# Gated attention in an encoder kernel: the gate weights in a tile of their own, loaded early, and the log decays written ahead of the copies of k

## The chip, the cores and the metric

One core of a Trainium2 chip runs the whole program in one launch. The metric is the device time of one execution in microseconds (us), the median of several runs. TensorE is written PE below, VectorE DVE, ScalarE ACT, GpSimd POOL and SyncE SP. SP issues nearly all transfers, from one queue, in the order in which they stand in it.

## The reference

The reference is a two-layer encoder on 512 tokens of width 1024. Layer 0 has two mixers side by side: a bidirectional diagonal state-space layer (S5) with a gated linear unit behind it, and a bidirectional gated linear attention (GLA) with four heads. Both read one combined input projection, and their outputs go through one output projection. A mixture of experts (MoE) follows. Layer 1 is a windowed attention with its own MoE. The change is in the GLA's log decays:

```python
def gla_bidir(q, k, v, go, lr, gate_w, gate_b, norm_g):
    ...
    z = jnp.einsum('blsr,srk->blsk', lrf, gate_w.astype(f32)) + gate_b.astype(f32)
    log_a = (jax.nn.log_sigmoid(z) / GLA_TAU).reshape(bsz, L, 2, GLA_HEADS, GLA_DK)
    ...
def gla_chunked(q, k, v, log_a, strict):
    bc = jnp.cumsum(log_a, axis=2)
    b_last = bc[:, :, -1]
    qd = q * jnp.exp(bc)
    kd = k * jnp.exp(-bc)
    ...
    kc = k * jnp.exp(b_last[:, :, None] - bc)
```

## The kernel before

`mixer0` (line 177) holds layer 0's two mixers. Its work is cut into steps (one projection block, one S5 direction, one stage of the GLA), and the string `STEPS0` (line 45) names them in the order in which they are written. A list scheduler then orders the instructions of PE, DVE, ACT and SP by priorities that follow the written order and by its own estimates of when each could run; POOL keeps the written order. So a step that is written elsewhere also moves its neighbours on each engine. Tiles are taken from pools of SBUF by a tag and a count of buffers (`a8`); a new tile of a tag that is full waits for the last readers of the buffer that it takes over. PSUM banks go round in the same way.

The steps that matter here:

- `loads` (step N) loads two rows broadcast over 128 partitions: `glb`, the bias of the S5's gated unit, and `ng`, the GLA's norm gain. Its transfers stand in SP's queue between the load of `Dv` and the projection weights `wr` of the second block of 256 columns.
- `lowrank` (L) computes `lrT`, the gate's low-rank input, transposed.
- `gla_a` (line 822) is a generator that the steps A1 to A5 advance. Its first stage takes `gt4`, four matrices in one tile: number 0 is `WG`, the gate weights of both directions with the bias as a row under them; number 1 is the mask that makes cumulative sums. DVE clears `WG` (L834), and four small transfers fill it (L837, L838). The second stage copies q into `q2` (four copies on ACT, four on DVE), then k into `k2` (eight copies on ACT, L858). The next stage makes the log decays: a matmul of `lrT` with `WG` for each of four blocks of tokens, |z| on ACT (L868, in four pieces), exp (L870) and ln (L871) over all four, and `la = min(z, 0) - ln(1 + exp(-|z|))` on DVE (L873). Then come the cumulative sums as matmuls of `la` with the mask, the exponentials (L887 to L889), and the scaled `kd`, `lt` and `q` on DVE (L893 to L895).
- The S5 runs between these: `s5_ht_min` makes `HT` (L646) and `Min` (L652, four ACT copies out of PSUM banks that PE filled with transposes of `PB`); `s5_y` makes the outputs `yg` of one half in two ACT operations (L785) and stores them to DRAM scratch `yd` in two transfers (L788). `Min` and `yg` are of the same tag (s5, four buffers).
- `glu_w` (E1) loads the gated unit's weights `glw`; `glu` reads `yd` back into `cat` (L800) and runs the unit (L817 to L819). The output projection's weights `wo` (L987) stand behind that read in SP's queue.

Of the kernel before, what the change touches and what calls it, by code (L numbers as in the profile page):

```python
# [39 lines left out]
def row_bcast(ap1d, n, parts=128, off=0):  # L40
    return bass.AP(tensor=ap1d.tensor, offset=ap1d.offset + off, ap=[[0, parts], [1, n]])
# [1 line left out]


STEPS0 = (
    "R1 R2 X R3 u0 RE R4 L RA p0a Q m0a u1 p1a UL p0b c0a U V c1a h0a x0a h1a m1a W c0b Ha F c1b r0a p1b N x1a G r1a K A1 A2 A3 A4 m0b ya h0b h1b x0b x1b r1b Hb m1b r0b A5 D1 yb D2 E1 E2")
STEPS1 = (
# [64 lines left out]
class Net:  # L112
# [64 lines left out]
    def mixer0(self, A, B1):  # L177
        nc, tc = self.nc, self.tc
        V, S, G = nc.vector, nc.scalar, nc.gpsimd
        i = self.i  # L180
        zone = dict(tt=0, ht=0, ph=0, phb=0, wlr=0, lrT=0, cs=1, U=1, B0=1, xtB=2, AA=2, C2=2, s5=3, wr=4, t1=4, t2=4,
                    wh=4, wl=4)
        W = i["ab_w_in"][0].rearrange("(p k) n -> p k n", k=8)
# [3 lines left out]
        def a8(shape, name, tag="s5", dt=F32, parts=128):  # L187
            return A[zone.get(tag, 5)].tile([parts] + list(shape), dt, name=name, tag=tag, bufs=bufs.get(tag, 1))
# [121 lines left out]
        qk = self.half("qk", [4, 512])  # L310
        self.XSm = self.half("XS", [2, 2, 8, 64])

        def qk_done(c):
            def f(m, b):
                j = (c - 512) // 128 + m
                S.activation(qk[:, j], b, AF.Copy, scale=0.125 if j < 2 else 1.0)
            return f

        T = {}
# [6 lines left out]
        def proj(c, how, done):  # L326
            blocks[c] = raw(c)
            prep(c)
            V.tensor_tensor(pend[c][1], blocks[c], pend[c][0].bitcast(F32), op=OP.subtract)
            how(c, done)  # L330
# [26 lines left out]
        def v_done(c):  # L357
            v = tile("v", [4, 512], "v", "t1")

            def f(h, b):  # L360
                S.activation(v[:, 2 * h:2 * h + 2, c - 1024:c - 768], b, AF.Copy)
            return f

        def go_done(c):
# [3 lines left out]
                S.activation(go[:, 2 * h:2 * h + 2, c - 1536:c - 1280], b, AF.Silu)  # L368
            return f

        def ga():
            if "ga" not in T:
                T["ga"] = self.gla_a(qk, T["lrT"])
            next(T["ga"])

        def gb():
# [3 lines left out]

        def loads():
            T["cat"] = [self.half(f"cat{h}", [4, 512]) for h in range(2)]
            T["glb"], T["ng"] = a8([512], "glb", "glb"), a8([512], "ng", "ng")
            nc.sync.dma_start(T["glb"], row_bcast(i["s5_glu_b"], 512))
            nc.sync.dma_start(T["ng"], row_bcast(i["gla_norm_g"], 512))

        def glu_w():
            T["glw"] = glw = a8([4, 512], "glw", "wh")
            nc.sync.dma_start(glw, i["s5_glu_w"][0].rearrange("(p k) n -> p k n", k=4))
            T["glu"] = self.glu(T["cat"], glw, T["glb"])  # L390
            next(T["glu"])
# [3 lines left out]
            "RE": lambda: self.s5_eph(), "RA": lambda: self.s5_pow(), "X": xsplit,  # L395
            "u0": lambda: uproj(0), "u1": lambda: uproj(256), "UL": uload,
            "Q": lambda: proj(512, transposed, qk_done(512)), "K": lambda: proj(768, transposed, qk_done(768)),
            "L": lowrank, "U": chunks,
            "V": lambda: proj(1024, tok_major, v_done(1024)), "W": lambda: proj(1280, tok_major, v_done(1280)),
            "G": lambda: proj(1536, tok_major, go_done(1536)), "F": lambda: proj(1792, tok_major, go_done(1792)),  # L400
            "A1": ga, "A2": ga, "A3": ga, "A4": ga, "A5": ga, "N": loads, "D1": gb, "D2": gb, "E1": glu_w,
            "E2": lambda: next(T["glu"], None)}
        for hf, c in enumerate("ab"):
# [415 lines left out]
            V.tensor_mul(cat[0][:, t], cat[0][:, t], b)  # L819


    def gla_a(self, qk, lrT):

        nc, a8, i = self.nc, self.a8, self.i
        V, S, G = nc.vector, nc.scalar, nc.gpsimd

        def tt(o, x, y, op):
            V.tensor_tensor(o, x, y, op=op)

        def tile8(name, tag):  # L830
            return self.a8([4, 512], name, tag)
        gt4 = tile8("gt4", "wl")
        WG = gt4[:, 0].rearrange("p (h d e) -> p h d e", h=4, d=2)
        V.memset(WG, 0.0)  # L834
        for d in range(2):
            gw = i["gla_gate_w"][0, d].rearrange("r (h e) -> r h e", h=4)
            nc.sync.dma_start(WG[16 * d:16 * d + 16, :, d, :], gw)  # L837
            nc.sync.dma_start(WG[32:33, :, d, :], i["gla_gate_b"][0, d].rearrange("(h e) -> h e", h=4)[None])  # L838

        mk = gt4[:, 1].rearrange("p (m i) -> p m i", m=4)  # L840
        for j, op in enumerate((OP.is_ge, OP.is_le, OP.is_lt, OP.is_gt)):
            V.tensor_scalar(mk[:, j], self.jp, 0.0, None, op0=op)
        V.memset(mk[0:64, :, 64:128], 0.0)
        V.memset(mk[64:128, :, 0:64], 0.0)
        yield
        q2, k2 = tile8("q2", "wr"), tile8("k2", "xtB")
        n = 0
        for m in range(4):
            if m == 2:
                yield  # L850
            dst = q2 if m < 2 else k2
            for s in range(2):
                for d in range(2):
                    o, x = dst[64 * d:64 * d + 64, 2 * (m % 2) + s], qk[64 * s:64 * s + 64, m]
                    e = "SSSSVVVVSSSSSSSS"[n]
                    n += 1
                    if e == "S":
                        S.activation(o, x, AF.Copy)  # L858
                    else:
                        (V if e == "V" else G).tensor_copy(o, x)  # L860
        yield

        la, lt = tile8("la", "xtA"), tile8("lt", "xtA")
        zs = []
        for t in range(4):
            b = self.bank("p" if t < 2 else "b")
            self.mm(b, lrT[:, 128 * t:128 * t + 128], gt4[:, 0])
            S.activation(lt[:, t], b, AF.Abs)  # L868
            zs.append(b)
        S.activation(lt, lt, AF.Exp, scale=-1.0)  # L870
        S.activation(lt, lt, AF.Ln, bias=1.0)  # L871
        for t in range(4):
            V.scalar_tensor_tensor(la[:, t], zs[t], 0.0, lt[:, t], op0=OP.min, op1=OP.subtract)  # L873
        yield
        dec = self.small([32], "dec", z=5)
        kc, kd = lt, tile8("kd", "wh")
        for h in range(4):
            bs = []
            for m in range(2):
                b = self.bank("p")  # L880
                for t in range(4):
                    for d in range(2):
                        o = 128 * h + 64 * d
                        self.mm(b[64 * d:64 * d + 64, 128 * t:128 * t + 128], la[:, t, o:o + 64], mk[:, 2 * m + d])
                bs.append(b)
            b, r = bs
            S.activation(kd[:, h], b, AF.Exp, scale=-1.0 / 16)  # L887
            S.activation(b, b, AF.Exp, scale=1.0 / 16)
            S.activation(kc[:, h], r, AF.Exp, scale=1.0 / 16)  # L889
            for d in range(2):  # L890
                a, c = slice(64 * d, 64 * d + 64), 63 - 63 * d
                S.activation(dec[a, 8 * h:8 * h + 8][:, ::1 - 2 * d, None], b[a].rearrange("p (n c) -> p n c", c=64)[:, :, c:c + 1], AF.Copy)
            V.tensor_tensor(kc[:, h], kc[:, h], k2[:, h], op=OP.mult)  # L893
            V.tensor_tensor(q2[:, h], q2[:, h], b, op=OP.mult)
            V.tensor_tensor(kd[:, h], kd[:, h], k2[:, h], op=OP.mult)  # L895
        self.gl = q2, kc, kd, dec
        yield
# [1299 lines left out]
```

## Time and profile before

| what | value |
|---|---|
| median of 3 runs | 1537.61 us (1532.17, 1537.61, 1541.21) |
| the profiled execution | 1535.62 us, its span 1533.8 us |
| mean granted TensorE clock | 0.957 |
| PE busy | 1378.0 us, 90% of the span |
| DVE, ACT, POOL busy | 658.8, 374.6, 138.1 us |
| DMA, mean over the span | 301 GB/s |

The span runs from the first to the last instruction of the profiled execution, whose own time is 1.8 us longer. The shares of busy time are means over stages that have different limits: the mixers of layer 0 lie in the first 275 us, the first MoE behind them, then layer 1 and the second MoE. The granted clock says how much of its full speed TensorE had in a stretch.

### The profile page before, as it was taken

To read this page: it belongs to the slowest core of one execution; us is meant where nothing else is said; L and a number is where in the kernel's file an instruction comes from. 1 tells how busy PE (TensorE), PEld (TensorE's weight loads), DVE (VectorE), ACT (ScalarE), POOL (GpSimd) and SP (SyncE) were. 2 spreads that over 40 slices of the span, in tenths; PEclk is the share of its full clock that TensorE was granted. 3 is DMA by queue.
4 is the path that set the end of the run, shared out by engine and by line. 5 is a ranking of instruction groups with operands and counts; after the bars stand their busy time and mean duration, and the time that the engine had idled before them with its cause. 6 is when DMAs were issued, how large, how long until landed. Compare 5 with 4: busy or idle time off the path is not lost. (4 is left out here: it accounts for less than half of the span.)

```text
span 1533.8 us, 21149 instructions
## 1 busy us (share of the span) xinstructions
PE 1378.0 (90%) x8291; PEld 796.5 (52%) x8291; DVE 658.8 (43%) x1518; ACT 374.6 (24%) x689; POOL 138.1 (9%) x116
## 2 busy tenths in 40 slices
PE   7999669999979999879797999999988999979785
PEld 6988557884524355324245875665534354424242
DVE  6988796562221322212125467664221223212125
ACT  3233736321101111001014566532101011101012
POOL 1000004320000000000005343021000000000003
PEclk9999989999999999989998999999999999999897
DMA  6234126477999999999995136478999999999993
GB/s 166 83 84 90 43 35 218 185 278 300 393 420 422 421 422 423 419 419 422 419 399 185 30 105 172 147 288 315 413 405 422 423 420 421 421 419 420 419 415 136
DMA packets 106167, 461.61 MB, mean 301 GB/s; under 512 B 17738, under 2 KB 43818, under 8 KB 63440
## 3 DMA queue, kind: packets, MB, share of 16 engines
q1 hardware_dynamic: 105952, 460.11, 76.9%
q8 instruction: 67, 1.10, 0.3%
q14 instruction: 36, 0.29, 0.1%
q0 software_dynamic: 112, 0.10, 0.0%
HBM read 455.46 MB, written 4.72 MB: 300 GB/s over the span
## 5 line engine op out<-in xcount | busy, mean ns | idle before, releaser
L122 PE MATMUL b<-w,xe 128*64 128x512 f32 (+1 forms) x2144 | 401.2, 618 | 38.6 <-DMA w<-in_moe_w_dram 33.8
L122 PEld LDWEIGHTS b<-w,xe 128*64 128x64 f32 (+1 forms) x2144 | 116.0, 127 | 291.1 <-issue 219.0
L122 PE MATMUL b<-w,hT 128*64 128x512 f32 (+1 forms) x1088 | 217.7, 624 | 34.6 <-DMA w<-in_moe_w_dram 33.1
L1637 DVE TENSOR_TENSOR x<-x,b 128x512 f32<-128x512 f32 x176 | 112.2, 681 | 151.8 <-PE b L122 149.5
L122 PEld LDWEIGHTS b<-w,hT 128*64 128x64 f32 (+1 forms) x1088 | 59.5, 128 | 178.1 <-issue 105.6
L1607 DVE SCALAR_TENSOR_TENSOR yl<-b,gs,yh 128x512 fp32r<-128x512 f32 x52 | 39.0, 750 | 217.6 <-ACT yh L1606 217.1
L122 PE MATMUL b<-S,xh 128*128 128x256 f32 x448 | 113.3, 293 | 0.3 <-DVE S L1510 0.3
L122 PE MATMUL b<-S,xl 128*128 128x256 f32 x448 | 111.5, 288 | 0.0
L1583 DVE TENSOR_TENSOR hs<-hs,b 128x512 f32<-128x512 f32 x26 | 17.9, 688 | 203.5 <-PE b L122 203.5
L122 PEld LDWEIGHTS b<-S,xh 128*128 128x128 f32 x448 | 88.5, 198 | 10.4 <-issue 9.9
L1606 ACT ACTIVATE yh<-b,gs 128x512 fp32r<-128x512 f32 x52 | 35.8, 688 | 234.9 <-PE b L122 226.6
L122 PEld LDWEIGHTS b<-S,xl 128*128 128x128 f32 x448 | 88.6, 198 | 0.0
L122 PE MATMUL b<-yh,GT 128*128 128x512 f32 x208 | 88.2, 429 | 0.4 <-ACT yh L1606 0.4
L1591 ACT ACTIVATE hT<-b 128x512 f32<-128x512 f32 x26 | 15.6, 599 | 292.7 <-PE b L136 292.7
L122 PE MATMUL b<-yl,GT 128*128 128x512 f32 x208 | 80.9, 396 | 0.7 <-DVE yl L1607 0.6
L1582 ACT ACTIVATE hs<-b 128x512 f32<-128x512 f32 x26 | 15.6, 599 | 200.7 <-PE b L122 200.7
L122 PEld LDWEIGHTS b<-yh,GT 128*128 128x128 f32 x208 | 39.2, 189 | 46.6 <-issue 35.0
L122 PE MATMUL b<-wh,xt 128*128 128x256 f32 x384 | 55.6, 297 | 3.2 <-ACT wh L171 3.2
L122 PEld LDWEIGHTS b<-wh,xt 128*128 128x128 f32 x384 | 51.3, 203 | 4.4 <-ACT wh L171 3.6
L122 PE MATMUL b<-xTh,spa 128*128 128x512 f32 x160 | 51.6, 394 | 0.5 <-ACT scv L1927 0.5
L1891 POOL TENSOR_TENSOR spv<-cw,spv 128x2048 fp32r<-128x2048 f32 x1 | 4.6, 4552 | 465.0 <-ACT spv L1890 465.0
L1551 DVE TENSOR_REDUCE gs<-b 64x1 f32<-64x2 f32 (+2 forms) x64 | 10.1, 157 | 83.8 <-PE b L122 82.0
(407 smaller groups left out, 2055.1 us busy)
## 6 DMA issues: line engine op xcount, KB each, us to landing
w<-in_moe_w_dram SPq DMA_DIRECT2D x288, 1024.0 KB, 19.8
w<-in_moe_w_dram SPq DMA_DIRECT2D x46, 2048.0 KB, 21.8
bias<-Ld SPq DMA_DIRECT2D x32, 384.0 KB, 3.4
wr<-in_ab_w_in_dram SPq DMA_DIRECT2D x8, 1024.0 KB, 6.1
x<-in_x_dram SPq DMA_DIRECT2D x8, 512.0 KB, 7.2
wo<-in_ab_w_out_dram SPq DMA_DIRECT2D x2, 2048.0 KB, 15.9
cw<-in_c_w_in_dram SPq DMA_DIRECT2D x2, 2048.0 KB, 9.8
cwo<-in_c_w_out_dram SPq DMA_DIRECT2D x16, 256.0 KB, 5.4
```

What stands on the lines that cost most here:

```text
L122: self.nc.tensor.matmul(o, l, r, start=start, stop=stop)
L1551: nc.vector.tensor_reduce(gt[o:o + n], b[o:o + n, 2 * a:2 * a + 2], axis=AX.X, op=OP.add)
L1582: nc.scalar.activation(hs, b1, AF.Silu)
L1583: nc.vector.tensor_mul(hs, hs, b3)
L1591: self.nc.scalar.activation(hT, b.rearrange("p (k s) -> p k s", k=4), AF.Copy)
L1606: nc.scalar.activation(yh[:, j], b[j], AF.Copy, scale=gs)
L1607: nc.vector.scalar_tensor_tensor(yl[:, j], b[j], gs, yh[:, j].bitcast(F32), op0=OP.mult, op1=OP.subtract)
L1637: V.tensor_add(xs, xs, b)
L1891: eng.tensor_tensor(dst[:, 1], raw, dst[:, 0].bitcast(F32), op=OP.subtract)
```

## The change

The gate weights get a tile of their own, which takes the one buffer of tag `glb`. A new step `g`, written directly behind `L`, clears it on POOL and issues its four transfers. The load of `glb` moves from step N to step E1, where it takes over that buffer. `gla_a` no longer clears or loads anything, and its log decays are written ahead of the eight copies of k instead of behind them. What is computed is unchanged.

```diff
 STEPS0 = (
-    "R1 R2 X R3 u0 RE R4 L RA p0a Q m0a u1 p1a UL p0b c0a U V c1a h0a x0a h1a m1a W c0b Ha F c1b r0a p1b N x1a G r1a K A1 A2 A3 A4 m0b ya h0b h1b x0b x1b r1b Hb m1b r0b A5 D1 yb D2 E1 E2")
+    "R1 R2 X R3 u0 RE R4 L g RA p0a Q m0a u1 p1a UL p0b c0a U V c1a h0a x0a h1a m1a W c0b Ha F c1b r0a p1b N x1a G r1a K A1 A2 A3 A4 m0b ya h0b h1b x0b x1b r1b Hb m1b r0b A5 D1 yb D2 E1 E2")
...
+        def gate_w():
+            T["WG"] = a8([512], "WG", "glb")
+            WG = T["WG"].rearrange("p (h d e) -> p h d e", h=4, d=2)
+            G.memset(WG, 0.0)
+            for d in range(2):
+                gw = i["gla_gate_w"][0, d].rearrange("r (h e) -> r h e", h=4)
+                nc.sync.dma_start(WG[16 * d:16 * d + 16, :, d, :], gw)
+                nc.sync.dma_start(WG[32:33, :, d, :], i["gla_gate_b"][0, d].rearrange("(h e) -> h e", h=4)[None])
...
         def loads():
-            T["glb"], T["ng"] = a8([512], "glb", "glb"), a8([512], "ng", "ng")
-            nc.sync.dma_start(T["glb"], row_bcast(i["s5_glu_b"], 512))
+            T["ng"] = a8([512], "ng", "ng")
             nc.sync.dma_start(T["ng"], row_bcast(i["gla_norm_g"], 512))
...
         def glu_w():
+            T["glb"] = a8([512], "glb", "glb")
+            nc.sync.dma_start(T["glb"], row_bcast(i["s5_glu_b"], 512))
             T["glw"] = glw = a8([4, 512], "glw", "wh")
...
-    def gla_a(self, qk, lrT):
+    def gla_a(self, qk, lrT, WG):
         gt4 = tile8("gt4", "wl")
-        WG = gt4[:, 0].rearrange("p (h d e) -> p h d e", h=4, d=2)
-        V.memset(WG, 0.0)
-        for d in range(2):
-            gw = i["gla_gate_w"][0, d].rearrange("r (h e) -> r h e", h=4)
-            nc.sync.dma_start(WG[16 * d:16 * d + 16, :, d, :], gw)
-            nc.sync.dma_start(WG[32:33, :, d, :], i["gla_gate_b"][0, d].rearrange("(h e) -> h e", h=4)[None])
...
+        stack(0, q2, "SSSS")
+        stack(1, q2, "VVVV")
         yield
         la, lt = tile8("la", "xtA"), tile8("lt", "xtA")
         for t in range(4):
             b = self.bank("p" if t < 2 else "b")
-            self.mm(b, lrT[:, 128 * t:128 * t + 128], gt4[:, 0])
+            self.mm(b, lrT[:, 128 * t:128 * t + 128], WG)
             S.activation(lt[:, t], b, AF.Abs)
...
             V.scalar_tensor_tensor(la[:, t], zs[t], 0.0, lt[:, t], op0=OP.min, op1=OP.subtract)
+        yield
+        stack(2, k2, "SSSS")
+        stack(3, k2, "SSSS")
         yield
```

How the instructions moved is shown at three places. The names end in a number that differs between the two programs; `b` is a PSUM bank, and the line numbers behind line 368 are shifted in the changed kernel.

First, SP's queue at the start of the program, where the second block of projection weights `wr` is loaded. Before:

```order
L230 DMA Dv<-in_s_d_dram 16x8x1 x4
L384 DMA glb<-in_s_glu_b_dram 128x512
L385 DMA ng<-in_gla_norm_g_dram 128x512
L210 DMA wr_579<-in_ab_w_in_dram 128x8x256
L296 DMA ud<-ut 128x2x256 x2
```

Changed:

```order
L230 DMA Dv<-in_s_d_dram 16x8x1 x4
L378 DMA WG<-in_gla_gate_w_dram 16x4x64
L379 DMA WG<-in_gla_gate_b_dram 1x4x64
L378 DMA WG<-in_gla_gate_w_dram 16x4x64
L379 DMA WG<-in_gla_gate_b_dram 1x4x64
L394 DMA ng<-in_gla_norm_g_dram 128x512
L210 DMA wr_585<-in_ab_w_in_dram 128x8x256
L296 DMA ud<-ut 128x2x256 x2
```

Four small transfers stand where one load of 256 KB stood, ahead of `wr`. Their old place, behind the eight transfers of the first `Mi`, holds `glb` now.

Second, ACT from the last copy of a projection out of PSUM (L316) to the first `Min`, with the semaphores that each instruction waits on (PE_49 is PE's, DMAHW4 and DMAHW5 are two of the eight that transfers use in turn). Before:

```order
L316 ACTIVATE qk<-b_1630 128x512 [waits PE_49]
L858 ACTIVATE k_1694<-qk 64x512 [waits Activation_49]
L858 ACTIVATE k_1694<-qk 64x512 x3
L868 ACTIVATE lt<-b_1713 128x512 [waits PE_49]
...
L868 ACTIVATE lt<-b_1722 128x512 [waits PE_49]
...
L785 ACTIVATE yg_1741<-b_1742 128x4x8x16 [waits PE_49]
L785 ACTIVATE yg_1741<-b_1768 128x4x8x16
L646 ACTIVATE HT_1796<-b_1797 128x512 [waits PE_49]
L652 ACTIVATE Min_1815<-b_1816 128x512 [waits PE_49,Pool_49]
```

Changed:

```order
L316 ACTIVATE qk<-b_1634 128x512 [waits PE_49]
L871 ACTIVATE lt<-b_1704 128x512 [waits PE_49]
L859 ACTIVATE k_1693<-qk 64x512 [waits Activation_49]
L859 ACTIVATE k_1693<-qk 64x512
L871 ACTIVATE lt<-b_1710 128x512 [waits PE_49]
L859 ACTIVATE k_1693<-qk 64x512 x2
L871 ACTIVATE lt<-b_1713 128x512 [waits PE_49]
L871 ACTIVATE lt<-b_1707 128x512 [waits PE_49]
...
L796 ACTIVATE yg_1740<-b_1767 128x4x8x16
L657 ACTIVATE HT_1795<-b_1796 128x512 [waits PE_49]
L663 ACTIVATE Min_1814<-b_1815 128x512 [waits DMAHW4_49,DMAHW5_49,PE_49,Activation_49]
```

The pieces of |z| stand between the last copies of k instead of behind them. The first `Min` of this group takes the buffer of the `yg` just above it and waits for that `yg`'s two stores; before, the second group of `Min`, further down, waited for them. On DVE the two L619 products of the next `PB` moved from behind the four `la` to ahead of them. On PE three of the four `WG` matmuls follow the last projection matmul, and the fourth stands among the S5's output matmuls.

Third, ACT where the S5's second `yg` and the GLA's states `St` meet. Before:

```order
L785 ACTIVATE yg_2306<-b_2333 128x4x8x16
L939 ACTIVATE St_2197<-sts_2296 64x896
L940 ACTIVATE St_2197<-sts_2296 64x896
L965 ACTIVATE on,ss<-b_2375 128x128 x4
L965 ACTIVATE on,ss<-b_2413 128x128 x4
```

Changed:

```order
L945 ACTIVATE St_2196<-sts_2295 64x896
L946 ACTIVATE St_2196<-sts_2295 64x896
L796 ACTIVATE yg_2305<-b_2332 128x4x8x16
L971 ACTIVATE on,ss<-b_2374 128x128 x4
L971 ACTIVATE on,ss<-b_2412 128x128 x4
```

The last part of the second `yg`, on which its two stores wait, now stands behind the last pair of `St` copies.

## Rows read from the trace of the kernel before

**Rows 1.** The page: PE's busy time and share; GB/s moved in 40 slices.
```profile
PE   1378.0 (90%) x8291; PEld 796.5 (52%) x8291; DVE 658.8 (43%) x1518; ACT 374.6 (24%) x689; POOL 138.1 (9%) x116
...
GB/s 166 83 84 90 43 35 218 185 278 300 393 420 422 421 422 423 419 419 422 419 399 185 30 105 172 147 288 315 413 405 422 423 420 421 421 419 420 419 415 136
```
**Rows 2.** PE's timeline: start, us, engine, line, operation, count, idle before and releaser.
```profile
163.79 5.14 PE L122 MATMUL b<-gt,lrT 128*128 128x512 f32 x8 [8.29 <-DMA gt<-in_gla_gate_b_dram]
```
**Rows 3.** Windows: length, busy time per engine, granted clock, DMA share, GB/s.
```profile
163.80:169.00 5.20, 5.20 (x10) 2.17 (x12) 4.91 (x7) 1.82 (x4) 0.00 (x0) 0.72 0.00 0
...
280.00:300.00 20.00, 20.00 (x106) 17.01 (x105) 12.05 (x18) 4.14 (x5) 5.98 (x3) 1.00 0.30 110
```
**Rows 4.** ACT's timeline from the copies of k to the first exponential.
```profile
160.69 2.55 ACT L858 ACTIVATE k<-qk 64x512 f32<-64x512 f32 x4
165.88 0.60 ACT L868 ACTIVATE lt<-b 128x512 f32<-128x512 f32 x1 [2.64 <-PE b L122]
167.25 0.60 ACT L868 ACTIVATE lt<-b 128x512 f32<-128x512 f32 x1 [0.78 <-PE b L122]
168.11 0.60 ACT L868 ACTIVATE lt<-b 128x512 f32<-128x512 f32 x1 [0.26 <-PE b L122]
...
174.10 1.91 ACT L871 ACTIVATE lt<-lt 128x2048 f32<-128x2048 f32 x1
...
177.32 1.09 ACT L785 ACTIVATE yg<-b 128x512 f32<-128x512 f32 x2
...
181.08 2.06 ACT L652 ACTIVATE Min<-b 128x512 f32<-128x512 f32 x4 [2.18 <-PE b L136]
...
184.45 0.60 ACT L887 ACTIVATE kd<-b 128x512 f32<-128x512 f32 x1
```
**Rows 5.** DVE's timeline over the same stretch and a little beyond.
```profile
168.15 0.67 DVE L674 TENSOR_TENSOR CS<-CS,phb 128x496 f32<-128x496 f32 x1
176.04 2.48 DVE L873 SCALAR_TENSOR_TENSOR la<-b,lt 128x512 f32<-128x512 f32 x4 [7.23 <-ACT lt L871]
...
180.71 2.35 DVE L619 TENSOR_TENSOR Mo<-C,AA 128x1024 f32<-128x1024 f32 x2
...
185.29 0.68 DVE L895 TENSOR_TENSOR kd<-kd,k 128x512 f32<-128x512 f32 x1
...
194.66 0.69 DVE L895 TENSOR_TENSOR kd<-kd,k 128x512 f32<-128x512 f32 x1 [1.02 <-ACT kd L887]
```
**Rows 6.** DMA issues between 155 and 200 us: KB each, us from issue to landing.
```profile
yd<-yg SPq DMA_DIRECT2D x2, 256.0 KB, 3.7
gt<-in_gla_gate_w_dram SPq DMA_DIRECT2D x2, 16.0 KB, 2.2
```
**Rows 7.** SP's timeline, the early loads and the gate weights: start and length of each issue.
```profile
24.21 0.43 SPq L384 DMA_DIRECT2D glb<-in_s_glu_b_dram  x1
...
25.22 0.58 SPq L210 DMA_DIRECT2D wr<-in_ab_w_in_dram  x1
...
159.51 0.66 SPq L837 DMA_DIRECT2D gt<-in_gla_gate_w_dram  x1
```
**Rows 8.** ACT's timeline, the split of the second block of weights.
```profile
35.68 1.91 ACT L171 ACTIVATE wh<-wr 128x2048 fp32r<-128x2048 f32 x1 [5.93 <-DMA wr<-in_ab_w_in_dram]
```
**Rows 9.** DMA issues between 0 and 60 us, the slowest kind to land.
```profile
Cn<-in_s_c_re_dram SPq DMA_DIRECT2D x4, 128.0 KB, 11.8
```
**Rows 10.** ACT's timeline where the second yg and St meet.
```profile
237.23 0.60 ACT L785 ACTIVATE yg<-b 128x512 f32<-128x512 f32 x1
237.85 0.95 ACT L939 ACTIVATE St<-sts 64x896 f32<-64x896 f32 x1
```
**Rows 11.** SP's timeline: the output projection's weights.
```profile
247.94 1.06 SPq L987 DMA_DIRECT2D wo<-in_ab_w_out_dram  x2
```
**Rows 12.** ACT's timeline: their first use.
```profile
259.07 3.91 ACT L999 ACTIVATE hi<-wo 128x1024 fp32r<-128x1024 f32 x4 [2.23 <-DMA wo<-in_ab_w_out_dram]
```
**Rows 13.** PE's timeline: the first work behind the gated unit.
```profile
269.62 3.37 PE L136 MATMUL b<-ident,cat 128*128 128x128 f32 x16 [3.36 <-DVE cat L819]
```

More of the change, by code (lines that the diff above doesn't have):

```diff
@@ L369, in go_done @@
             return f
+        def gate_w():
[6 more added lines that the diff above has]
+                nc.sync.dma_start(WG[32:33, :, d, :], i["gla_gate_b"][0, d].rearrange("(h e) -> h e", h=4)[None])
         def ga():
             if "ga" not in T:
-                T["ga"] = self.gla_a(qk, T["lrT"])
+                T["ga"] = self.gla_a(qk, T["lrT"], T["WG"])
             next(T["ga"])
@@ L397, in mixer0 @@
             "Q": lambda: proj(512, transposed, qk_done(512)), "K": lambda: proj(768, transposed, qk_done(768)),
-            "L": lowrank, "U": chunks,
+            "L": lowrank, "g": gate_w, "U": chunks,
             "V": lambda: proj(1024, tok_major, v_done(1024)), "W": lambda: proj(1280, tok_major, v_done(1280)),
@@ L846, in gla_a, with stack @@
         q2, k2 = tile8("q2", "wr"), tile8("k2", "xtB")
[L847 to L851, printed above, removed]
+        def stack(m, dst, engines):
             for s in range(2):
@@ L854, in gla_a @@
                     o, x = dst[64 * d:64 * d + 64, 2 * (m % 2) + s], qk[64 * s:64 * s + 64, m]
-                    e = "SSSSVVVVSSSSSSSS"[n]
-                    n += 1
-                    if e == "S":
+                    if engines[2 * s + d] == "S":
                         S.activation(o, x, AF.Copy)
                     else:
-                        (V if e == "V" else G).tensor_copy(o, x)
+                        V.tensor_copy(o, x)
+        stack(0, q2, "SSSS")
+        stack(1, q2, "VVVV")
         yield
```

## The prediction, made before the changed kernel had run

> **What bounds the kernel now.** I read the page first. PE is busy 90% of the span, and the slices with 414 to 423 GB/s [rows 1] are the two MoE stages, which stream their weights as fast as the transfers go. The change lies in front of the first of them, in the mixers of layer 0, so the question is what a time saved there is worth at the mixers' end, and whether the MoE passes it on. It should: between 280 and 300 us the transfers are busy 30% of the time and PE all of it [rows 3], so the MoE's first weights are there already and wait for their users. A shift of the mixers' end then moves the end of the kernel by as much.
>
> Next I read PE's timeline for what the gate weights cost. PE stands still for 8.29 us until the last of the four small transfers has landed, and then spends 5.14 us on the four decay matmuls [rows 2] at a granted clock of 0.72 [rows 3]. The cause is the place of the transfers: SP issues the first at 159.51 [rows 7] and the weights land 2.2 us after an issue [rows 6].
>
> Then the other two engines, since idle time of PE counts only where the others wait for it. ACT copies k until about 163.2 and then waits for PE before each of the four pieces of |z|: 2.64, 0.78 and 0.26 us, and the fourth like the third, 3.94 us in all [rows 4]. Exp, ln and the gelu behind them are a chain on ACT alone. DVE is out of work from 168.82 and waits 7.23 us for ln [rows 5]; from there on it hardly stops, with one gap of 1.02 us at 194.66 [rows 5]. So the chain behind the decays is ACT's until ln, then DVE's.
>
> **What the change removes.** With `WG` loaded at the start, PE goes straight on from the projections, and |z| no longer waits. ACT has the same copies and the same four pieces to do, in another order, so ln ends 3.9 us earlier, at 172.1 instead of 176.0. DVE has also taken two L619 products of 2.35 us into the hole in front of `la`: they run from 168.8 to 171.2, `la` from 172.1 to 174.6, and the products for `Mo` that began at 180.71 [rows 5] can begin there. That is 6.1 us gross on DVE. On ACT it is the same if nothing else holds it: `Min` waits another 2.18 us on PE's transposes [rows 4], which now run ahead of the decay sums, and 3.94 + 2.18 is 6.1.
>
> **What it adds.** Three terms.
>
> First, ACT's first `Min` takes the buffer of the `yg` just above it and waits for its stores. The pair of `yg` starts at 173.4, 3.9 earlier than 177.32 [rows 4], and ends at 174.5; the stores are issued then and about 0.6 later, and one takes 3.7 us to land [rows 6]. So `Min` starts at 178.8 instead of 181.08, and `kd` (L887) at 182.2 instead of 184.45 [rows 4]. Of the 6.1 us 2.3 are left on ACT. DVE gets its first `kd` (L895) at about 182.8 instead of 185.29 [rows 5], 2.5 earlier; its order changes here too, and part of the 1.02 us that it idles later [rows 5] goes as well. I take 2.8 for DVE, between 2.3 (no more than ACT) and 3.5 (all of that gap).
>
> Second, the last part of the second `yg` stands behind a pair of `St` copies of 0.95 us each [rows 10], so it comes 1.9 us later relative to its neighbours: 237.23 plus 1.9 minus 2.8 is 0.9 earlier than before, no more. Behind it hang its stores, the read of `yd`, and in SP's queue the output projection's weights, issued at 247.94 [rows 11]. ACT waits 2.23 us for those [rows 12], with the gated unit's sigmoids queued behind it, and PE waits 3.36 us for the unit's last product [rows 13]. So at the output projection 0.9 us of the gain is left, although PE and DVE come there 2.8 earlier. If PE's own matmuls end that wait instead, up to 2.8 is left.
>
> Third, the early queue. Four issues take the place of one in front of `wr`. By the row they take some 0.66 us each [rows 7], about 2.8 with the gaps between them, in place of some 0.5 for `glb` [rows 7]: `wr` is issued 2.3 us later. In return the 256 KB of `glb` are not ahead of it; at the 166 GB/s of the page's first slice [rows 1] they take 1.6 us. ACT waits 5.93 us for this `wr` [rows 8], so nothing covers a delay. The cost lies between -1.6 and +2.3, and I take the difference, +0.7.
>
> [...]
>
> At nothing I cost three things. POOL's memset of `WG`: POOL is busy 9% of the span [rows 1], and the transfers wait behind others in SP's queue anyway. The DVE memset that goes (L834): DVE was early there and waited 7.23 us in front of `la` [rows 5]. `glb` behind the first `Mi`: it is read past 259, behind the weights `wo` [rows 12]; only if it held back `yd`'s stores, which are queued behind it, would it count, with its issue of 0.43 [rows 7].
>
> **Sum.** -2.8 + 1.9 + 0.7 = -0.2 us. From the profiled execution's 1535.62 that is 1535.4; the median of the runs lies 2.0 above that execution, so 1537.4 as a median. About 0.5% (7.7 us) is what a measurement of this kernel can tell from no change, so the forecast is: no change.
>
> **The rivals.**
>
> *A, most of the gain arrives.* Either the stores land before `Min` needs the buffer, or PE and not the weights `wo` ends the wait at the output projection. For it: the last product for which PE waits there is made from PE's own last matmuls of the unit, by way of DVE and ACT, and that path comes 2.8 earlier. Against it: 3.7 us to landing and 2.23 us of waiting are measured. It gives 2.8 to 6.1 off, 1534.8 to 1531.5. Chance 0.25.
>
> *B, PE's gap is the price.* The gap on PE closes and everything behind it comes up by 8.3 us; the decay matmuls also run at full clock, 5.2 us at 0.72 [rows 3] being worth 1.4. Together 9.7, so 1527.9. For it: PE is the busiest engine by far. Against it: DVE's chain has only 6.1 us to give. [...] Chance 0.10.
>
> *C, slower, by the early queue.* The gate weights are rows of 256 bytes, and the small-piece loads of `Cn` in the same stretch took 11.8 us to land [rows 9], against 2.2 for the gate weights on a quiet queue [rows 6]. If they crowd the engines in front of `wr`, ACT's split of it [rows 8] and the projections move back. From 2.3 us of delay, less the 0.9 left of the gain, it is +1.4 (1539.0); with all of 9.6 us more (11.8 - 2.2) it is +8.7 (1546.3). It decides from 0.9 us of delay on. Against it: they are 34 KB together, `Cn`'s loads are 128 KB each. Chance 0.10, six in ten of it above 7.7.
>
> *D, the decays wait as before*, for the low-rank input or a bank instead of the weights, and the change does nothing: 1537.6. Chance 0.05: `lrT` is made by step L, right in front of the early loads.
>
> **How the numbers follow.** The forecast has the rest, 0.50. Faster by over 0.5%: all of B and 0.04 of A, where A's 6.1 meets a lucky early queue: 0.14. Slower: 0.06, from C. The rest, 0.80, within. The range goes down to A's 6.1 with 1.6 of early gain, 1529.9, and up to the middle of C, 1537.6 + 5 = 1542.6; B and the upper half of C stay out.
>
> **What would show it.** Right: no wait of PE in front of the `WG` matmuls; |z| without idle time; `la` at about 172; idle time of some 4 us on ACT in front of the first `Min`, released by the `yd` stores; the second `yg` behind the last `St`; `wo` issued less than 1 us earlier. Wrong: the output projection's transposes 2.5 us earlier or more (A), or ACT's second split of weights later than 38 (C).

## The result, and the profile after

The changed kernel takes **1548.62 us** as a median (five runs, 1545.3 to 1549.88), the kernel before 1537.61: a ratio of 1.0079 [1.0053, 1.0106]. It is slower by 11.0 us, where no change was forecast (1537.4, range 1529.9 to 1542.6).

The page of the changed kernel, PE's busy time and granted clock (answers to [rows 1]):

```profile
span 1546.8 us, 21152 instructions
...
PE 1391.5 (90%) x8291; PEld 806.3 (52%) x8291; DVE 663.0 (43%) x1517; ACT 374.4 (24%) x689; POOL 138.4 (9%) x117
...
PEclk9999896999999999989998999999999999999898
```

PE does the same 8291 matmuls and is busy 13.5 us longer. That alone speaks against a new wait as the whole loss: the matmuls themselves take longer somewhere. The profiled execution is the median one, 1548.62 us around a span of 1546.8.

**What came out as forecast.** PE's timeline where the gate weights were waited for [rows 2]:

```profile
152.92 2.74 PE L122 MATMUL b<-WG,lrT 128*128 128x512 f32 x6
...
156.39 1.13 PE L122 MATMUL b<-WG,lrT 128*128 128x512 f32 x2
...
171.23 2.82 PE L136 MATMUL b<-ident,PB 128*128 128x128 f32 x12 [7.75 <-ACT yg L796]
```

The 8.29 us in front of the gate matmuls are gone. A gap of 7.75 us stands instead in front of `ident,PB`, which needs the bank that ACT's first `yg` is read from. ACT's timeline over the same stretch [rows 4], then DVE's [rows 5]:

```profile
161.74 1.08 ACT L871 ACTIVATE lt<-b 128x512 f32<-128x512 f32 x2
...
167.36 1.91 ACT L874 ACTIVATE lt<-lt 128x2048 f32<-128x2048 f32 x1
...
170.58 1.08 ACT L796 ACTIVATE yg<-b 128x512 f32<-128x512 f32 x2
...
176.54 2.07 ACT L663 ACTIVATE Min<-b 128x512 f32<-128x512 f32 x4 [4.38 <-DMA yd<-yg]
...
179.92 0.60 ACT L893 ACTIVATE kd<-b 128x512 f32<-128x512 f32 x1
```
```profile
169.30 2.48 DVE L876 SCALAR_TENSOR_TENSOR la<-b,lt 128x512 f32<-128x512 f32 x4 [1.27 <-ACT lt L874]
...
180.55 0.69 DVE L901 TENSOR_TENSOR kd<-kd,k 128x512 f32<-128x512 f32 x1 [4.19 <-ACT kd L893]
```

The pieces of |z| have no idle time, and `Min` waits 4.38 us for the stores of `yd`. One execution starts its work earlier or later than another, so I count from the first copy of q on ACT (148.58 us before, 145.98 after; 142.3 to 148.8 in the traces of all kernels of this document): `la` comes 4.1 us earlier, DVE's first `kd` 2.1.

The early queue, SP's issues and ACT's second split [rows 7, 8]:

```profile
23.25 0.65 SPq L378 DMA_DIRECT2D WG<-in_gla_gate_w_dram  x1
...
25.41 0.64 SPq L379 DMA_DIRECT2D WG<-in_gla_gate_b_dram  x1
...
26.63 1.06 SPq L210 DMA_DIRECT2D wr<-in_ab_w_in_dram  x1
```
```profile
33.06 1.92 ACT L171 ACTIVATE wh<-wr 128x2048 fp32r<-128x2048 f32 x1 [5.45 <-DMA wr<-in_ab_w_in_dram]
```

The four issues cost what was reckoned, yet the second split comes 15.49 us after the first, not 16.82 as before: `wr` is there 6.4 us after its issue against 10.4. The traces of the experiments below agree: the mean is 16.0 us over the seven kernels with the early gate weights and 17.0 over the eleven without. The copies of q follow the second split by 112.9 us in both kernels here, but by 109.5 to 114.2 over all traces, so how much of this gain of 1.0 to 1.3 us arrives is not shown.

**Where the time goes.** ACT's end of the same step [rows 10] and PE beside it; of PE the rows of the kernel before come last:

```profile
230.89 0.95 ACT L945 ACTIVATE St<-sts 64x896 f32<-64x896 f32 x1 [0.77 <-DVE sts L943]
...
233.79 0.95 ACT L946 ACTIVATE St<-sts 64x896 f32<-64x896 f32 x1
234.76 0.60 ACT L796 ACTIVATE yg<-b 128x512 f32<-128x512 f32 x1
242.09 0.28 ACT L971 ACTIVATE on<-b 128x128 f32<-128x128 f32 x1 [6.73 <-PE b L122]
```
```profile
228.98 4.46 PE L122 MATMUL b<-q,kd 64*128 64x128 f32 x40
235.41 1.22 PE L122 MATMUL b<-q,kd 64*128 64x128 f32 x4 [1.97 <-ACT yg L796]
236.56 0.80 PE L122 MATMUL b<-v,AT 128*128 128x128 f32 x2
237.29 0.70 PE L122 MATMUL b<-St,q 128*64 128x128 f32 x4
```
```profile
235.31 3.48 PE L122 MATMUL b<-q,kd 64*128 64x128 f32 x44
238.72 0.49 PE L122 MATMUL b<-v,AT 128*128 128x128 f32 x2
239.14 0.44 PE L122 MATMUL b<-St,q 128*64 128x128 f32 x4
```

The second `yg` stands behind the last `St` pair, as forecast. But the sixth bank of `q,kd` products (of the matmul instructions, eight fill a bank) is the bank from which this `yg` reads: PE waits 1.97 us for it, and every product behind the wait is slow, 0.80 and 0.70 us where the kernel before has 0.49 and 0.44. The windows (length, busy time of PE, PEld, DVE, ACT, POOL, granted clock, DMA share, GB/s) say why; first of the change, then two of the kernel before:

```profile
230.00:235.00 5.00, 3.39 (x34) 3.04 (x32) 4.17 (x13) 4.16 (x6) 0.00 (x0) 1.00 0.02 3
235.00:240.00 5.00, 4.59 (x19) 3.03 (x20) 0.34 (x1) 0.36 (x1) 0.00 (x0) 0.54 0.43 105
240.00:245.00 5.00, 5.00 (x24) 3.01 (x24) 0.89 (x2) 1.58 (x8) 0.93 (x1) 0.50 0.87 221
...
250.00:255.00 5.00, 5.00 (x23) 3.09 (x21) 4.24 (x8) 0.00 (x0) 0.91 (x2) 0.50 1.05 398
255.00:260.00 5.00, 5.00 (x29) 4.17 (x27) 2.08 (x4) 3.55 (x12) 1.88 (x2) 0.57 1.05 387
260.00:265.00 5.00, 5.00 (x32) 3.67 (x31) 2.62 (x8) 2.48 (x11) 0.57 (x1) 1.00 1.03 410
```
```profile
240.00:245.00 5.00, 5.00 (x40) 3.09 (x40) 0.90 (x2) 1.58 (x8) 1.03 (x1) 1.00 0.57 153
...
255.00:260.00 5.00, 5.00 (x26) 4.07 (x23) 3.36 (x15) 2.41 (x9) 2.38 (x15) 1.00 1.04 385
```

Behind the wait the granted clock is 0.50 for some 24 us (from 235.4 to 259.3 by these shares; windows of 1 us show 0.50 in each from 236 to 259 and 1.00 from 260 on), although PE is busy all that time; before, the clock is 1.00 from 232 to 269. Counted from the copies of q, the first `on` is 2.7 us late, the first product behind the gated unit's `cat` 8.7, the output projection's first copy on ACT 8.2. That copy, of the change and of the kernel before:

```profile
276.39 0.60 ACT L1016 ACTIVATE xh<-b 128x512 fp32r<-128x512 f32 x1 [1.53 <-PE b L136]
```
```profile
270.75 0.60 ACT L1010 ACTIVATE xh<-b 128x512 fp32r<-128x512 f32 x1 [1.99 <-PE b L136]
```

### The profile page after: what moved, and what is told of

Same layout as the page of the kernel before. It is cut to its first block, busy times and chain, and to the rows that moved or that the text cites. A ratio compares the mean times of both kernels' runs of the same rounds, so it can differ in the third digit from the quotient of the medians.

```text
span 1546.8 us, 21152 instructions
## 1 busy us (share of the span) xinstructions
PE 1391.5 (90%) x8291; PEld 806.3 (52%) x8291; DVE 663.0 (43%) x1517; ACT 374.4 (24%) x689; POOL 138.4 (9%) x117
## 5 line engine op out<-in xcount | busy, mean ns | idle before, releaser
L122 PE MATMUL b<-w,xe 128*64 128x512 f32 (+1 forms) x2144 | 396.9, 609 | 40.2 <-DMA w<-in_moe_w_dram 35.4
L122 PE MATMUL b<-w,hT 128*64 128x512 f32 (+1 forms) x1088 | 225.4, 654 | 34.4 <-DMA w<-in_moe_w_dram 32.9
L122 PEld LDWEIGHTS b<-S,xh 128*128 128x128 f32 x448 | 88.0, 196 | 10.9 <-issue 10.3
L122 PEld LDWEIGHTS b<-yh,GT 128*128 128x128 f32 x208 | 39.2, 189 | 46.2 <-issue 33.8
```

The lines of the kernel that those rows point to most:

```text
L122: self.nc.tensor.matmul(o, l, r, start=start, stop=stop)
```

## The experiments

Theory T: the wait for the second `yg`'s bank halves PE's clock, and that is the loss. Its rival L (W in e3's text): the late `yg`, its stores and the weights `wo` behind them are the loss, and the clock is by the way. A third, Q, stands in the first texts: the early queue or the wait of `Min` for the stores is the loss. "Half clock" is a stretch at a granted clock of 0.50, looked for between 230 and 265 us; shorter ones elsewhere, which the kernel before has too (221 to 232 us, 269 to 273), are not counted. Medians of the kernel before beside these runs were 1536.2 (e1 to e4), 1537.0 (e5 to e12) and 1537.1 (e13 to e16).

| run | kernel | median, us (runs) | ratio to before | PE's wait, us | half clock, about |
|---|---|---|---|---|---|
| e1 | change, `yg` first | 1534.1 (12) | 0.9987 [0.9972, 1.0003] | 0.60 | none |
| e3 | change, wait filled | 1534.9 (12) | 0.9988 [0.9971, 1.0006] | 0.20 | none |
| e4 | change, `yg` between the last two `St` | 1542.3 (10) | 1.0032 [1.0005, 1.0060] | 1.43 | 233 to 247 |
| e9 | gate weights alone | 1545.0 (6) | 1.0053 [1.0034, 1.0073] | 1.97 | 237 to 260 |
| e2 | before, `yg` behind `St` | 1541.1 (12) | 1.0029 [1.0008, 1.0051] | none | none |
| e5 | e2, 1 us later | 1540.0 (12) | 1.0025 [1.0005, 1.0045] | none | none |
| e6 | e5, filled | 1540.4 (12) | 1.0025 [1.0007, 1.0044] | none | none |
| e13 | before, wait made | 1541.0 (10) | 1.0021 [0.9997, 1.0044] | 1.07 | 244 to 265 |
| e14 | before, wait made | 1544.3 (8) | 1.0050 [1.0031, 1.0070] | 2.04 | 237 to 258 |
| e15 | e14, filled | 1539.6 (10) | 1.0007 [0.9990, 1.0025] | none | none |
| e16 | before, wait made | 1549.7 (7) | 1.0071 [1.0044, 1.0097] | 3.02 | 242 to 263 |

**e1 and e4: move the `yg`.** The last `yg` goes in front of the last `St` pair, or between its two copies (e4, where only the second copy moves).

```diff
+            if h == 3:
+                break
             S.activation(St[h // 2][0:64, h % 2, 1:8], st[0:64, 0:7], AF.Copy)
...
+        with self.tc.issue_after(self.yg_last.ins):
+            S.activation(St[1][0:64, 1, 1:8], st[0:64, 0:7], AF.Copy)
+            S.activation(St[1][64:128, 1, 0:7], st[64:128, 6::-1], AF.Copy)
```


> The changed kernel with one thing undone: the second part of the last yg stands ahead of the last pair of St copies on ACT again, as before the change. Theory T (PE waits 1.97 us for this yg at 233.4, because the next bank of q,kd is the one that yg is read from; the granted clock falls to 0.5 with that wait and stays there for 22 us): the wait goes or shrinks to a few tenths, the clock between 235 and 258 is 1.0 again, and the time comes to 1533 to 1537, some 11 to 15 below the changed kernel's 1548.6, since the 2.5 to 3.4 us that were won up to 230 are then kept. Rival Q (the loss comes from the early queue, the wait of Min for the stores of yd or the later issue of x and of the MoE's weights): the time stays at 1546 to 1549.

> The changed kernel with the second part of the last yg between the two St copies of the last pair: it ends one copy (0.96 us) earlier, so PE's wait falls from 1.97 to about 1.0 us. Theory T says that the time follows the clock and not the wait: either 1547 to 1549 with 22 us at half clock (a wait of 1 us is enough), or 1534 to 1538 with none. A time in between, 1540 to 1545, with a half-clock stretch of some 10 us would speak for a drop whose length follows the wait. Rival Q: 1547 to 1549.

e1 gives 14.5 us back, with the early queue and the wait of `Min` (4.40 us) as they were, so Q falls. e1 is as fast as the kernel before, within the interval, not faster. e4 lies between, and its ten runs spread from 1529.0 to 1549.8: the same program, some executions as quick as e1, some as slow as the change. PE waits 1.43 us where 1.0 was expected, because in this program (and in e1) this `yg` hands its bank to the fifth `q,kd` group, which comes earlier. The profiled execution, one of the quick ones (1536.4), has 14 us at half clock and comes to the output projection 4.8 us late, counted from the copies of q; those start at 142.3 us, earliest of all traces, which hides it in the time. What the slow ones lose is not seen.

**e3: fill the wait.** `yg` stays late; the four products of the fifth bank are done five times, the order of everything else is the change's (further edges hold it there).

```diff
-                for h in range(4):
+                for h in list(range(4)) * (5 if (t, d) == (2, 0) else 1):
                     self.mm(b[:, 128 * h:128 * h + 128], kd[ds, h, ts_], q2[ds, h, ts_])
```


> The changed kernel with PE kept at work where it waited: the four matmuls of the bank ahead of the waiting one are done five times (sixteen matmuls more, about 2.5 us, the same values into the same bank); yg stays late, the order of every engine stays. Theory T, that the clock and not the wait itself costs the time: the clock stays at 1.0 from 235 to 258, PE loses 0.5 us more than by waiting, and the time falls by about 11 to 1536 to 1538. Rival W (what costs is that everything behind the late yg is late): 1548 to 1550.

PE's timeline and two windows of e3:

```profile
233.00 6.94 PE L958 MATMUL b<-q,kd 64*128 64x128 f32 x68 [0.20 <-ACT yg L796]
239.87 0.49 PE L968 MATMUL b<-v,AT 128*128 128x128 f32 x2
```
```profile
240.00:245.00 5.00, 5.00 (x38) 3.14 (x38) 0.86 (x2) 1.59 (x8) 0.00 (x0) 1.00 0.53 132
...
255.00:260.00 5.00, 5.00 (x28) 3.80 (x27) 3.43 (x11) 3.05 (x10) 2.24 (x9) 1.00 1.04 390
```

(The wait of 0.20 us is for another bank, that of this `yg`'s first part.) Work that nobody needs makes the kernel 13.7 us faster than the change and brings it back to the time of the kernel before. The first `on` is as late as in the change (95.9 us after the copies of q, against 96.1), `wo` is issued later (101.2 against 99.4), and the first product behind the gated unit's `cat` comes 7.3 us earlier. Rival L has no room for that.

**e2, e5, e6: the late `yg` in the kernel before.** The second `yg` is ordered behind the last `St` copy (e2, PE's order held); that copy is done twice, so that `yg` comes another 1 us later (e5); and e5 with the fill of e3 (e6).

```diff
+            with self.tc.issue_after(self.st_last.ins) if hf and jb else nullcontext():
                 nc.scalar.activation(ygv[:, 4 * jb:4 * jb + 4],
```


> The kernel before with this one thing added: the second part of the last yg behind the last pair of St copies, every other engine in its old order. It ends 1.9 us later, at about 239.8, and PE comes to the bank that it holds at about 238.5. Theory T: PE waits some 1.3 us there, and if a wait of this length is enough, the clock halves for 20 us as in the changed kernel: 1546 to 1550. Theory T with a longer wait needed: 1538 to 1540. Rival Q: 1538 to 1540, and no stretch at half clock behind 238.

> The kernel before, with the late yg of run e2 and one St copy done twice ahead of it (the same values), so that the yg ends another 0.96 us later and PE's wait in front of the bank is some 2 us long, as in the changed kernel. Nothing else of the change is in it. Theory T (the wait brings the clock down): half clock from about 240 to 258 in the profile and 1546 to 1550, about 10 above the kernel before, although no more than 2 to 3 us of work or waiting were added. Rival (the drop needs something else of the changed kernel, e2 at 1541 being all that the order is worth): 1540 to 1543 with the clock at 1.0.

> The same late yg as in e5, and PE kept at work in front of it, as in e3: the four matmuls ahead are done five times, some 2.5 us. Theory T: the clock stays at 1.0, and of e5's loss only the lateness of yg and the sigmoids behind it is left: 1537 to 1541. Rival (lateness is what costs): as e5.

Theory T's numbers for e2 and e5 failed, for a plain reason: the programs as built give the sixth `q,kd` group another bank than the one that this `yg` reads, so PE does not wait at all. In e5 it goes on to `v,AT` while this `yg` is still to come, and in e6 the fill has no wait to fill:

```profile
236.76 0.49 PE L962 MATMUL b<-v,AT 128*128 128x128 f32 x2
```
```profile
238.06 0.60 ACT L786 ACTIVATE yg<-b 128x512 f32<-128x512 f32 x1
```

So none of the three tests T. What remains of them is a price for lateness alone: 3.8 to 4.5 us by the ratios, each with an interval of some 3 us to either side, without a half clock behind `q,kd`.

**e9: one part of the change.** The gate weights early, and the text of the decays left behind the copies of k.

> The gate weights alone in their own tile and loaded ahead, the decays left behind the copies of k in the text. The order on every engine is that of the change but for one pair of k copies on ACT. Theory T (the second yg behind the last St pair makes PE wait some 2 us for its bank, and PE then runs at half clock): as the change, a wait of 1.9 to 2.1 us in front of the sixth bank of q,kd, granted clock 0.5 for 15 to 22 us behind it, 1545 to 1550. Rival (it takes the reordered copies of k as well): no wait, clock 1.0, 1534 to 1538.

The wait, the half clock and most of the loss are there. The reordered copies of k are not needed for it.

**e10, e11, e12: an edge the wrong way round.** In the kernel before, with the last `St` copy done twice (e10) or three times (e11, e12), and in e12 the four products of the fifth bank seven times.

```diff
+                if t == 0 and h == 0:
+                    self.tc.add_manual_dep(st_last.ins, q.ins.name, mybir.DependencyInfo(
+                        mybir.DependencyClass.Sync, mybir.DependencyReason.DATA), reason="order")
```


> The kernel before, in which PE's first v,AT product is made to wait for the last St copy, and that copy is done twice; the second yg and its stores stay where they were. PE has no work to put into the wait, which should be about 2.0 us. Theory T: granted clock 0.5 for 15 to 22 us behind it, as in the change, and 1543 to 1549 with nothing else late. Rival L (the change is slow because yg's stores and the weights behind them are late, the clock is by the way): at most the 2 us of the wait, 1537 to 1539.

> The same with the last St copy done three times: a wait of about 3.0 us. Theory T: half clock behind it, 1544 to 1550. Rival L: 1538 to 1540.

> The kernel with three copies, and in the wait PE does the four q,kd products of the fifth bank seven times instead of once (24 more matmuls of some 0.11 us, 2.6 us). All is as late as with three copies, but PE waits under 0.5 us. Theory T: clock 1.0 between 235 and 260 us, 1537 to 1541, at least 5 less than without the fill. Rival L: the same time as without the fill.

The edge as written holds the last `St` copy behind PE's product and not the product behind the copy. So PE waits nowhere, the clock stays at 1.00, and e10 (1539.5, 1.0021 [1.0005, 1.0036]) and e11 (1537.0, 1.0007 [0.9986, 1.0029]) say nothing about T. e12 says something else: its extra products fill no wait and make the first `on` 6.2 us later at full clock, and the kernel takes 1544.7 (1.0052 [1.0032, 1.0072]), 7.7 more, by the interval 5 to 11. In its trace 5.5 of the 6.2 us are left at the output projection's first copy. So most of a delay at this place can be passed on; that it always is, is not shown (e15 below).

**e13 to e16: the wait alone.** The edge turned round, PE's other products held in their places; every engine keeps the order of before, and `yg` its place. The last `St` copy is done once, twice or three times (e13, e14, e16); e15 is e14 with the fill of e3.

```diff
+            for _ in range(2 if h == 3 else 1):
+                st_last = S.activation(St[h // 2][64:128, h % 2, 0:7], st[64:128, 6::-1], AF.Copy)
...
+                if t == 0 and h == 0:
+                    self.tc.add_manual_dep(q.ins, st_last.ins.name, mybir.DependencyInfo(
+                        mybir.DependencyClass.Sync, mybir.DependencyReason.DATA), reason="order")
```


> The kernel before, PE's first v,AT product waiting for the last St copy (which it does not read), nothing else changed and every engine's order as before. From the rows of before (q,kd done at 238.7, the last St copy at 239.8) a wait of about 1.0 us. Theory T (a wait of PE at this place halves its clock for 15 to 22 us): between 1538, if so short a wait leaves the clock alone, and 1546, if it does not. Rival L (the second yg's stores and the weights behind them are what is late): at most 1 us, 1536 to 1538.

> The same with the last St copy done twice, so a wait of about 2.0 us, as long as the one in the change; yg and its stores are where they were before. Theory T: granted clock 0.5 for 15 to 22 us behind it and 1543 to 1549. Rival L: 1537 to 1540.

> e14's kernel, and PE does the four q,kd products of the fifth bank five times in place of once, which puts some 1.8 us of matmuls into the wait; v,AT starts when it does in e14. Theory T: a wait under 0.5 us, clock 1.0 between 235 and 265 us, 1537 to 1541, at least 4 us less than e14. Rival L: the time of e14 within 2 us.

> e14's kernel with the last St copy done three times, a wait of about 3.0 us. Theory T: half clock behind it, 1544 to 1550. Rival L: 1538 to 1541.

PE's timeline and windows of e14, and below them of e15 ("issue" stands where the profile shows no releaser; ACT's last `St` copy ends at 236.07, just before PE goes on); e14's first copy of the output projection stands between them:

```profile
230.64 3.48 PE L953 MATMUL b<-q,kd 64*128 64x128 f32 x44
236.16 0.46 PE L965 MATMUL b<-v,AT 128*128 128x128 f32 x2 [2.04 <-issue]
...
238.00 0.80 PE L965 MATMUL b<-v,AT 128*128 128x128 f32 x2
```
```profile
235.00:240.00 5.00, 3.84 (x20) 2.39 (x20) 0.24 (x3) 1.03 (x2) 0.00 (x0) 0.72 0.58 122
240.00:245.00 5.00, 5.00 (x24) 2.93 (x24) 2.02 (x6) 1.58 (x8) 1.04 (x1) 0.50 0.79 203
...
250.00:255.00 5.00, 5.00 (x24) 3.00 (x25) 3.27 (x7) 0.26 (x2) 1.26 (x1) 0.50 1.05 389
255.00:260.00 5.00, 5.00 (x34) 4.28 (x32) 3.34 (x8) 3.38 (x12) 1.01 (x1) 0.73 1.04 397
```
```profile
275.06 0.60 ACT L1020 ACTIVATE xh<-b 128x512 fp32r<-128x512 f32 x1 [1.58 <-PE b L136]
```
```profile
233.05 7.77 PE L953 MATMUL b<-q,kd 64*128 64x128 f32 x76
240.75 0.49 PE L965 MATMUL b<-v,AT 128*128 128x128 f32 x2
```
```profile
240.00:245.00 5.00, 5.00 (x43) 3.40 (x41) 0.73 (x1) 0.91 (x5) 0.00 (x0) 1.00 0.61 183
...
250.00:255.00 5.00, 5.00 (x42) 3.85 (x40) 4.89 (x11) 2.68 (x11) 1.49 (x2) 1.00 0.94 349
```

A wait of the change's length, put into the kernel before with nothing else late, costs 7.2 us (1544.3 against 1537.1; 7.7 by the ratio, 5 to 11 by its interval), three and a half times itself. Filled with matmuls it cannot be told from no loss (2.5 us by the medians, 1.1 by the ratio), although the fill came out longer than planned: `v,AT` starts 7.7 us behind the first `q,kd` in e15, 5.5 in e14, 3.4 in the kernel before. Of these 4.3 us 2.7 are left at the output projection's first copy, so part of a delay is taken up there.

The longer the wait, the more: 3.9 us for 1.07, 7.2 for 2.04, 12.6 for 3.02 by the medians (3.2, 7.7 and 10.9 by the ratios; e13's interval includes no change). The traces take this apart. From the first `q,kd` to the output projection's first copy the kernel before takes 35.4 us, e13 43.4, e14 44.4 and e16 45.3. That is 8.0, 9.0 and 9.9 more: each time the wait itself and 6.9 us on top, with a half clock of 20.5 us in all three. So in these three executions a longer wait cost only its own length more. e13 is not even: its runs go from 1534.2 to 1551.2, and the profiled one is the slowest. The clock granted over each whole run goes with this: 0.957 to 0.958 in its three quickest runs, 0.943 to 0.951 in its four slowest. It also parts the other kernels: 0.949 or 0.950 in all five runs of the change, 0.954 to 0.962 in all runs of e1 and e3.

T holds on both kernels. L does not carry the loss on either: in e3 `yg` and `wo`, in e15 the products behind the wait, are as late or later, and the loss is gone or too small to tell.

**e7 and e8: keep the gain and the clock.** e1, and the first `yg` in another buffer, so that `Min` no longer waits for its stores.

```diff
-        yg = a8([8, 128], f"yg{hf}", "s5")
+        yg = a8([8, 128], f"yg{hf}", "s5" if hf else "xtB")
```


> Run e1 (last yg ahead of the last St) with the first yg in a buffer of another tag (tt), so that Min no longer waits 4.4 us for the stores of yd. The scheduler then puts Min and the first kd ahead of this yg, with one table load more on ACT behind them. If the wait of Min holds back the chain, as I put it in the prediction, DVE's first kd comes 3 to 4 us earlier still, counted from the copies of q, and the time falls to 1530 to 1533; if that gain is lost again at the output projection, where PE waits for the gated unit, it stays at 1533 to 1536 like e1.

> As e7, with the first yg in the free second buffer of tag xtB: here the scheduler takes yg in two parts, the first already between exp and ln (one table load more), and Min behind the second. Min does not wait for the stores. If what Min waits for is worth anything at the end: 1530 to 1533; if not, 1533 to 1537.

e7 (buffer "tt"): 1535.6, 0.9988 [0.9971, 1.0005]; DVE's `kd` comes only 0.8 us earlier than in e1. e8 (buffer "xtB", in which the first `yg` also moves between the exponential and ln): **1530.5**, 0.9960 [0.9939, 0.9980]. That beats both kernels. The first `kd` is no earlier than in e7 (33.7 and 33.8 us after the copies of q, e1 34.6), so the wait of `Min` does not explain the 5 us between the two; which part of e8's new order does is open.

## Why the prediction was wrong, point by point

- **What bounds the kernel, and that a shift at the mixers' end is passed on:** right as far as the runs can tell. e14's trace has the output projection's first copy 8.8 us late, counted from the copies of q, and the median is 7.2 later; in e12 it is 5.5 and 7.7.
- **The gain, -2.8:** the mechanism held (|z| without idle time, `la` early, the `yd` stores in front of `Min` at 4.38 us where "some 4" were expected), the size is 2.1 at DVE's first `kd`, where ACT's share was put at 2.3. The gap of 1.02 us in front of DVE's third `kd` did shrink, to 0.32, but a new one of 0.31 stands ahead of it, and the third `kd` is 2.4 us earlier.
- **The early queue, +0.7:** wrong in sign at the second split, -1.3 in this pair of traces and -1.0 by the means. The issues were priced rightly; what fell was the time that `wr` took to land, from 10.4 to 6.4 us, with the 256 KB of `glb` no longer in front of it. That `glb` is the cause is argued: no run moved it alone, and the 1.6 us that it was priced at are less than the 4.0 gained. Rival C was not what happened.
- **The second `yg`, +1.9: this is the step that failed.** It said "Behind it hang its stores, the read of `yd`, and in SP's queue the output projection's weights", and priced that chain alone. On that chain it was nearly right: the weights `wo` were issued 0.1 us later, counted from the copies of q, where 0.9 earlier was forecast. But the PSUM bank that `yg` reads is also handed on, to PE's sixth `q,kd` bank. The prediction's own numbers hold the wait: the kernel before as built hands this bank on in the same way, `yg` is read out at 237.83 and PE wants the bank at about 238.5 (forty of the 44 instructions from 235.31), a margin (the cover) of 0.6 us. PE was to come 2.8 us earlier and `yg` only 0.9, so the cover was overdrawn by 1.3. Measured: PE 2.4 earlier, `yg` 0.1 later, a wait of 1.97. With the step undone the rest of the sum came out as no change: e1 has 1534.1 against 1536.2.
- **The price of a wait.** Had the wait been found, I would have put it in at its length, some 2 us, and still called it no change. e14 shows 7.2, because the products behind it run at a granted clock of 0.50 for 20.5 us in its trace (e15, filled and without that stretch, shows 2.5). The change, e14 and e16 show such a stretch behind a single wait, of 1.97, 2.04 and 3.02 us; behind the wait of 1.94 us for `XS` in the change, told of below, the clock is 1.00.
- **Rivals.** A and B assumed that only the size of the gain was open. B's gap did not close, it moved to `ident,PB` (7.75 us). The slower side had C alone, a queue at the start; the second split came at 33.06 and not later than 38, and the real loss sat some 80 us behind the gate matmuls (from 152.92 to 233.4).

The loss in numbers: the mixers' end is 8.2 us late, counted from the copies of q, which themselves come some 1 us earlier by the early queue. That is 7 of the 11 us. From the output projection's first copy to the end the profiled executions took between 1263.0 and 1271.3 us, whatever the kernel. The one of the kernel before is the shortest of all eighteen (1263.0) and that of the change the second longest (1270.4), so the other 4 us are not located. e9, with the same wait and the same half clock, lost 8.0.

## What to carry to other kernels

When a change makes one engine earlier and another not, list every buffer and PSUM bank that passes between them behind the change, and set the new distance against the cover that the old trace shows; here the bank's next writer, PE, waited 1.97 us for the late read of `yg`. Do not price a new wait of PE at its length alone, look at the granted clock behind it: 2.04 us of waiting cost 7.2 in e14 with 20.5 us at 0.50 behind it, and 2.5 by the medians when it was filled (e15), while behind the change's 1.94 us for `XS` the clock stayed at 1.00. A filler, or another order of a few instructions on the producing engine, can take such a loss back whole (13.7 and 14.5 us here). It did not make this change a gain: e1 and e3 are level with the kernel before.

## What the hardware showed that was not expected

- The clock does not fall at every wait of the same length. At 205.73 us the changed kernel waits 1.94 us for `XS`, and the clock stays at 1.00 (200 to 215 us); e1 has the same wait, with the same length, and there the products behind it take 3.63 us instead of 2.21, at 0.80 in the window from 205 to 210 and 0.85 from 210 to 215:

```profile
205.73 2.21 PE L122 MATMUL b<-XS,swap 128*128 128x512 f32 x4 [1.94 <-DVE XS L734]
```
```profile
208.06 3.63 PE L122 MATMUL b<-XS,swap 128*128 128x512 f32 x4 [1.94 <-DVE XS L734]
```

- One program seems to have both outcomes: e4 (1.43 us) and e13 (1.07 us) spread over 21 and 17 us, and in e13 the quick runs have the higher granted clock. The change and e14 spread over 5 and 9 us, the kernel before beside these runs over 12 to 16. What decides it in one execution was not tried.
- The clock stayed at 0.50 for 20 to 24 us in which PE was busy nearly throughout, behind waits of 1.07 (e13), 1.97 (the change), 2.04 (e14) and 3.02 us (e16). Behind e1's wait for `XS` it was some 3.5 us by the two shares. So the length of the wait did not set the length of the stretch; what did is open.
